# Start and end of a hybrid decoder block: meta rows on another queue, gain in two tiles, the 16-row tile one piece earlier, the last row in quarters

## The chip, the cores and the metric

The kernel runs on one core of one Trainium2 chip. The metric is the device time of one execution in microseconds; the median of three runs of the kernel before is 744.31 us (744.23 to 744.82). The engines are TensorE (PE; its weight loads are listed apart as PEld), VectorE (DVE), ScalarE (ACT), GpSimd (POOL) and SyncE (SP), which only issues transfers. ScalarE has a queue for issuing transfers as well (ACTq). What each engine executes stands in one fixed order; engines wait for each other through semaphores.

## The reference

One decoder block on 1024 tokens of width 1024, with 16 learned meta tokens in front (1040 rows):

```python
h = concatenate([meta, x])                           # 1040 x 1024
h_n = h * rsqrt(mean(h * h) + 1e-6) * norm_g
u, z, q, k, v, za, f, gp, ga = split(h_n @ w_in)     # 8 heads of 64
y_pool = causal_multiscale_pool(u) * silu(z)
y_attn = forgetting_attention(q, k, v, log_sigmoid(f + b)) * silu(za)
merged = sigmoid(gp) * (y_pool @ w_up_pool) + sigmoid(ga) * (y_attn @ w_up_attn)
out = rmsnorm(h + merged @ w_out, final_norm_g)[16:]
```

Everything is float32. The kernel forms each product as three products of high and low parts (`hh`, `hl` of the activations; `whi`, `wlo` of the weights).

## The kernel before, in words

Rows are handled in nine tiles of 128; tile 0 holds the 16 meta rows and the first 112 tokens, and tile 8 the last 16 rows. `norm_load` (L171) brings a tile in on SP's queue; for tile 0 it issues two loads, the tokens and then the meta rows. `norm_stat` (L182) squares a tile on ScalarE, with the sum read out, then `rstd_of` (L110) adds epsilon on VectorE (L113) and raises to the power -0.5 on GpSimd (L114). `norm_scale` (L187) multiplies by that and by the gain on VectorE, in two halves of 512 columns. The gain `norm_g` arrives as one row, `grow`, on ScalarE's queue (L380), and two products of TensorE with a row of ones spread it over 128 partitions into `gb`, one tile of two halves; four warm-up products stand before and one behind. `norm_t` (L192) transposes a tile on TensorE, eight times 128 columns, into `pt` or `pn` in PSUM: there are two `pt` buffers, used in turn, and one `pn`. ScalarE copies the result to `hh` (L212) and VectorE writes the difference to `hl` (L213). Tile 8 takes the short way at L197, L201 and L202: all eight transposes into one `pt` buffer.

The first head pair's q, k and v are then projected in four stretches of tokens, 0 to 256, 256 to 512, 512 to 768, 768 to 1040, in the order q, k, v each: pieces n = 0 to 11 (L431 on). A piece is 24 products in three groups of eight (`hh,whi`, `hl,whi`, `hh,wlo`, L152) into one of three `pj` buffers. Behind or within the pieces stand the remaining tiles' work: which tile is scaled after which piece (L456) and transposed after which (L448) is written out in two tables. For tile 8, square and scale are written behind piece n = 6 and the transposes inside v's piece n = 8, behind its first eight products. q's piece is taken out by four copies on ScalarE (`qa`, L241) and two differences on VectorE (`ql`, L245); k's by L263 and L266.

TensorE's order is the order of the code. At the start, up to L475, the order of the other engines is the code's too. Behind it a scheduler sets theirs. Attention, pooling, gates and output products follow; the last ones (L995) are added to `x` row by row.

At the end each of eight row tiles of 128 collects two halves: `arrive` (L1006) adds a product on VectorE (L1001), squares it on ScalarE (L1015) and sums on GpSimd (L1018, L1021). `store` (L1023) raises to the power on GpSimd (L1026), scales one half on VectorE (L1028) and one on ScalarE (L1031), and issues one transfer for each, on SP's and ScalarE's queue. Two `after` calls, which order without a wait, put each scale behind the last addition or square so far. For row 7 the last half arrives in two quarters of 256 columns, and rows 6 and 7 are stored behind it.

Of the kernel before, what the change touches and what calls it, by code (L numbers as in the profile page):

```python
# [8 lines left out]
F32 = mybir.dt.float32  # L9
# [5 lines left out]
D = 1024  # L15
# [37 lines left out]
def tile_hybrid_block(ctx, tc, x, meta, norm_g, w_in, b_forget, pool_w, pool_scale,  # L53
# [114 lines left out]
    gb = psG.tile([128, 2, 512], F32, name="gb")  # L168
    junk = gp.tile([128, D], F32, name="junk", tag="g")

    def norm_load(i):  # L171
        c0 = i * 128
        n = min(128, L - c0)
        xt = ap_.tile([128, D], F32, name="xt", tag="s", bufs=6)
        if i == 0:
            nc.sync.dma_start(xt[NM:], x2[:128 - NM, :])
            nc.sync.dma_start(xt[:NM], meta)
        else:
            nc.sync.dma_start(xt[:n], x2[c0 - NM:c0 - NM + n, :])
        return xt  # L180

# [5 lines left out]
    def norm_scale(xt, n, r):  # L187
        for j, (c0, c1) in enumerate(HALVES):
            nc.vector.scalar_tensor_tensor(xt[:n, c0:c1], xt[:n, c0:c1], r[:n], gb[:n, j],
# [189 lines left out]
    grow = ap_.tile([1, D], F32, name="grow", tag="t")  # L379
    nc.scalar.dma_start(grow, norm_g)  # L380
    nc.scalar.activation(junk[:1, :2], r32(onesr)[:1, :2], AF.Square)
    xts = {0: norm_load(0), 1: norm_load(1)}
# [7 lines left out]
    for j, (c0, c1) in enumerate(HALVES):  # L390
        nc.tensor.matmul(gb[:, j], r32(onesr)[:1], grow[:, c0:c1], start=True, stop=True)
# [27 lines left out]
    for i in range(2):  # L419
        norm_scale(xts[i], 128, norm_stat(xts[i], 128))  # L420
# [13 lines left out]
    for n, (kind, t0, t1) in enumerate(todo):  # L434
# [4 lines left out]
        elif kind == "k":  # L439
            run(k_piece(0, wk, t0, t1))  # L440
        else:
            g = v_piece(0, wv, t0, t1)
            if n == 8:
# [3 lines left out]
            run(g)  # L447
        i = {0: 2, 1: 3, 3: 4, 4: 5, 6: 6, 7: 7}.get(n)  # L448
# [7 lines left out]
        i = {1: 4, 2: 5, 4: 6, 5: 7, 6: 8}.get(n)  # L456
        if i is not None:
# [548 lines left out]
    def arrive(r, c0, ps):  # L1006
        part, add = plus(r, c0, ps)
        if r not in cnts:
# [6 lines left out]
        marks.append((add, nc.scalar.activation(sq[:, :ps.shape[-1]], part, AF.Square, scale=D ** -0.5,  # L1015
                                                accum_out=sss[r][:, n:n + 1])))
# [6 lines left out]
    def store(r, c):  # L1023
# [4 lines left out]
        after(nc.vector.scalar_tensor_tensor(o[:, a0:a1], xr[r][:, a0:a1], t, fgb[:, a0:a1],  # L1028
                                             op0=ALU.mult, op1=ALU.mult), marks[-1][0])
        nc.sync.dma_start(o2[rr, a0:a1], o[:, a0:a1])  # L1030
        after(nc.scalar.activation(o[:, b0:b1], xr[r][:, b0:b1], AF.Copy, scale=t), marks[-1][1])  # L1031
        nc.scalar.dma_start(o2[rr, b0:b1], o[:, b0:b1])
# [17 lines left out]
    for n in range(7):  # L1050
# [59 lines left out]
```

## Time and profile before

| | us |
|---|---|
| median of 3 runs | 744.31 |
| profiled execution, its own time | 743.96 |
| its span, first to last instruction | 742.2 |
| TensorE busy | 731.2 |
| first projection product starts | 12.11 |
| q's last piece (n = 9) starts | 46.87 |
| last output pass on VectorE starts | 737.69 |

The span is the time between the first and the last instruction that the profiler saw; the execution's own time has 1.76 us around it. A row of a timeline gives the start in us, the time until the last of the merged instructions ends, the engine, the line, the operation, output and inputs by the program's names, shapes, how many were merged and, in brackets, how long the engine stood idle before and what ended that. Starts of instructions that follow each other on an engine can lie up to 0.1 us before the end of the one ahead. Lines are those of the kernel before.

### The profile page before, as it was taken

Reading aid. Unit: us, or ns where it says so; the run is one execution under the profiler, and the core shown is the slowest. Engines: PE = TensorE matmul, PEld = TensorE weight load, DVE = VectorE, ACT = ScalarE, POOL = GpSimd, SP = SyncE. Lnnn points to the kernel's source line nnn. Section 1 sums busy time; section 2 is a strip of 40 time slices with the busy share of each in tenths; the row PEclk is TensorE's granted clock in tenths of the full one; section 3 lists DMA queues with packets and bytes.
Section 4 is the critical chain, followed back from the end, with each engine's and each line's share of the span. In section 5 each row is a group of like instructions: output and inputs, shape, how many; then the busy total and the mean of one; then the engine's idle time right before and its main releaser. Section 6 shows DMA issues by size and latency. Waiting matters only on the chain.

```text
span 742.2 us, 10619 instructions
## 1 busy us (share of the span) xinstructions
PE 731.2 (99%) x3686; PEld 622.7 (84%) x3686; DVE 533.2 (72%) x991; ACT 377.0 (51%) x736; POOL 332.8 (45%) x390
## 2 busy tenths in 40 slices
PE   8999999999999999999999999999999999999996
PEld 5997999988888898889988888888887888888885
DVE  5653577668779877688797687686288554997975
ACT  6662556446557545556563564452545322526445
POOL 4331235456426446345355383183348043606743
PEclk9999999999999999999999999999999999999998
DMA  9301132231312212222323223229375357360006
GB/s 301 88 15 43 29 86 86 62 98 23 95 48 60 80 50 90 78 53 55 94 66 86 80 80 92 72 81 309 95 201 212 142 200 240 116 224 1 1 0 227
DMA packets 76424, 75.35 MB, mean 102 GB/s; under 512 B 9665, under 2 KB 60865, under 8 KB 76370
## 3 DMA queue, kind: packets, MB, share of 16 engines
q1 hardware_dynamic: 74496, 69.95, 30.8%
q10 hardware_dynamic: 1874, 4.72, 1.7%
q8 instruction: 29, 0.48, 0.3%
q14 instruction: 25, 0.20, 0.1%
HBM read 55.58 MB, written 19.07 MB: 101 GB/s over the span
## 4 chain that ended last, share of the span: by engine, by line
PE 87%; DVE 5%; ACT 1%; issue 1%; POOLq 0%; POOL 0%; ACTq 0%
PE pj L152 65%; PE pj L995 8%; PE po L633 5%; PE ps L573 2%; PE ps L572 2%; PE pt L995 2%; PE pj L486 1%; DVE S L612 1%; DVE pl L617 1%; DVE ka L266 0%; PE pj L279 0%; DVE pt L603 0%; ACT S L581 0%; DVE mt L593 0%; ACT whi L140 0%
## 5 line engine op out<-in xcount | busy, mean ns | idle before, releaser
L124 POOL TENSOR_TENSOR wlo<-raw,whi 128x256 fp32r<-128x256 f32 x148 | 121.7, 852 | 192.5 <-ACT whi L140 96.1
L152 PE MATMUL pj<-hh,whi 128*128 128x512 f32 (+4 forms) x768 | 178.4, 360 | 0.6 <-ACT hh L201 0.3
L152 PE MATMUL pj<-hl,whi 128*128 128x512 f32 (+4 forms) x768 | 177.1, 359 | 0.0
L152 PE MATMUL pj<-hh,wlo 128*128 128x512 f32 (+4 forms) x768 | 174.4, 358 | 0.0
L152 PEld LDWEIGHTS pj<-hh,wlo 128*128 128x128 f32 x768 | 132.3, 188 | 18.1
L152 PEld LDWEIGHTS pj<-hh,whi 128*128 128x128 f32 x768 | 131.5, 188 | 18.7 <-ACT hh L201 0.5
L152 PEld LDWEIGHTS pj<-hl,whi 128*128 128x128 f32 x768 | 131.6, 188 | 17.7
L617 DVE TENSOR_TENSOR pl<-S,ph 128x512 fp32r<-128x512 f32 (+4 forms) x112 | 87.1, 792 | 19.3 <-ACT ph L616 18.8
L625 POOL TENSOR_TENSOR acc<-acc,S 128x272 f32<-128x272 f32 (+4 forms) x80 | 76.7, 958 | 11.2 <-ACT S L613 6.0
L581 ACT ACTIVATE S<-ps,negc 128x400 f32<-128x400 f32 (+2 forms) x96 | 49.3, 515 | 44.0 <-DVE S L579 35.7
L613 ACT ACTIVATE S<-S 128x512 f32<-128x512 f32 (+4 forms) x112 | 49.5, 478 | 33.7 <-DVE S L612 33.5
L616 ACT ACTIVATE ph<-S 128x512 fp32r<-128x512 f32 (+4 forms) x112 | 52.2, 480 | 15.8 <-PE po L633 14.4
L588 DVE TENSOR_TENSOR m<-m,S 128x272 f32<-128x272 f32 (+4 forms) x80 | 41.3, 517 | 23.8 <-ACT S L581 22.0
L140 ACT ACTIVATE whi<-raw 128x1024 fp32r<-128x1024 f32 x37 | 39.1, 1056 | 32.2 <-PE pj L152 27.8
L612 DVE TENSOR_TENSOR S<-S,pt 128x512 f32<-128x512 f32 (+4 forms) x112 | 51.9, 498 | 0.8
L836 DVE TENSOR_TENSOR rl<-pj,rl 128x512 f32<-128x512 f32 x32 | 22.0, 689 | 28.0 <-PE pj L152 28.0
L579 DVE SCALAR_TENSOR_TENSOR S<-ps,negc,mask 128x128 f32<-128x128 f32 (+2 forms) x72 | 23.7, 330 | 22.5 <-PE ps L573 22.3
L317 ACT ACTIVATE st<-pj 128x512 f32<-128x512 f32 x40 | 23.7, 593 | 28.1 <-PE pj L152 18.6
L633 PE MATMUL po<-pl,V 128*128 128x512 f32 (+4 forms) x112 | 37.6, 336 | 0.1
L573 PE MATMUL ps<-ql,ka 128*128 128x512 f32 (+4 forms) x112 | 37.5, 334 | 0.0
L572 PE MATMUL ps<-qa,ka 128*128 128x512 f32 (+4 forms) x112 | 36.0, 322 | 0.6 <-ACT S L581 0.5
L995 PE MATMUL pj<-opy 128*128 128x512 f32 (+1 forms) x168 | 36.3, 375 | 0.0
(187 smaller groups left out, 1134.2 us busy)
## 6 DMA issues: line engine op xcount, KB each, us to landing
raw<-in_w_in_dram SPq DMA_DIRECT2D x40, 512.0 KB, 3.9
sp_gp<-st SPq DMA_DIRECT2D x16, 256.0 KB, 2.0
sp_ga<-st SPq DMA_DIRECT2D x16, 256.0 KB, 2.0
rl<-sp_gp SPq DMA_DIRECT2D x8, 512.0 KB, 5.2
rl<-sp_ga SPq DMA_DIRECT2D x8, 512.0 KB, 4.5
W<-in_w_out_dram SPq DMA_DIRECT2D x8, 512.0 KB, 4.8
xr<-in_x_dram SPq DMA_DIRECT2D x8, 512.0 KB, 4.1
xt<-in_x_dram SPq DMA_DIRECT2D x7, 512.0 KB, 8.1
```

Source lines behind the costliest of these rows:

```text
L124: ins = nc.gpsimd.tensor_tensor(out[:, c:c + 256], x[:, c:c + 256], y[:, c:c + 256], op=op)
L152: nc.tensor.matmul(ps, a, b, start=(i == 0), stop=(i == len(seq) - 1))
L572: nc.tensor.matmul(ps[:kb, c0:], ka[:, k0:k0 + kb], qa[:, q0 + c0:q0 + 512], start=True, stop=False)
L573: nc.tensor.matmul(ps[:kb, c0:], ka[:, k0:k0 + kb], ql[:, q0 + c0:q0 + 512], start=False, stop=True)
L581: nc.scalar.activation(s[:kb, f0:], ps[:kb, f0:], AF.Identity, bias=nb_)
L612: nc.vector.tensor_tensor(s[:kb, c0:], s[:kb, c0:], self.pm[:kb, c0:], op=ALU.subtract)
L613: exps.append(nc.scalar.activation(s[:kb, c0:], s[:kb, c0:], AF.Exp))
L616: nc.scalar.activation(ph[:kb, c0:], s[:kb, c0:], AF.Copy)
L617: dves.append(nc.vector.tensor_tensor(pl[:kb, c0:], s[:kb, c0:], r32(ph[:kb, c0:]), op=ALU.subtract))
L625: nc.gpsimd.tensor_tensor(acc[:kb, c0:], acc[:kb, c0:], s[:kb, c0:], op=ALU.add)
L633: nc.tensor.matmul(self.po[:, c0:], v, r[:kb, c0:], start=(b == 0 and i == 0), stop=(b == self.nb - 1 and i == 1))
L995: nc.tensor.matmul(ps, pick(A_, k, p)[:, i * 128:(i + 1) * 128], pick(B_, k, q)[:, c0:c1], start=start and n == 0, stop=n == 11, skip_grou ...
```

## The change

It has five parts.

- The meta rows are loaded from ScalarE's queue, ahead of the gain row, instead of from SP's behind tile 0's tokens.
- The gain is spread into two tiles, so that a half waits for its own product alone.
- Tiles 0 and 1 take a new `norm_stat2`: half of the squares on ScalarE, half on VectorE, both sums added to epsilon in one instruction.
- Tile 8 is squared and scaled behind piece n = 5 with tile 7, and transposed inside k's piece n = 7 behind its first eight products.
- The last quarter of row 7 is squared on VectorE and not marked for the `after` order, and row 7 is stored in four quarters, one issued by ScalarE and three by SP.

```diff
-    gb = psG.tile([128, 2, 512], F32, name="gb")
+    gb = [psG.tile([128, 512], F32, name=f"gb{j}") for j in range(2)]
...
         if i == 0:
+            nc.scalar.dma_start(xt[:NM], meta)
             nc.sync.dma_start(xt[NM:], x2[:128 - NM, :])
-            nc.sync.dma_start(xt[:NM], meta)
...
+    def norm_stat2(xt, n):
+        ss = [sm.tile([128, 1], F32, name="ss") for _ in range(2)]
+        nc.scalar.activation(junk[:n, :512], xt[:n, :512], AF.Square, scale=D ** -0.5, accum_out=ss[0][:n])
+        nc.vector.scalar_tensor_tensor(junk[:n, 512:], xt[:n, 512:], 1.0 / D, xt[:n, 512:], op0=ALU.mult, op1=ALU.mult,
+                                       accum_out=ss[1][:n])
+        r = sm.tile([128, 1], F32, name="rstd", bufs=4)
+        nc.vector.tensor_scalar(r[:n], ss[0][:n], ss[1][:n], EPS, op0=ALU.add, op1=ALU.add)
+        nc.gpsimd.tensor_tensor(r[:n], r[:n], epsp[:n], op=ALU.pow)
+        return r
...
-            nc.vector.scalar_tensor_tensor(xt[:n, c0:c1], xt[:n, c0:c1], r[:n], gb[:n, j],
+            nc.vector.scalar_tensor_tensor(xt[:n, c0:c1], xt[:n, c0:c1], r[:n], gb[j][:n],
...
+    xts = {0: norm_load(0)}
     nc.scalar.dma_start(grow, norm_g)
     nc.scalar.activation(junk[:1, :2], r32(onesr)[:1, :2], AF.Square)
-    xts = {0: norm_load(0), 1: norm_load(1)}
+    xts[1] = norm_load(1)
...
-        norm_scale(xts[i], 128, norm_stat(xts[i], 128))
+        norm_scale(xts[i], 128, norm_stat2(xts[i], 128))
...
         elif kind == "k":
-            run(k_piece(0, wk, t0, t1))
-        else:
-            g = v_piece(0, wv, t0, t1)
-            if n == 8:
+            g = k_piece(0, wk, t0, t1)
+            if n == 7:
                 for _ in range(KO):
                     next(g)
                 norm_t(8, xts[8], ntok(8))
             run(g)
+        else:
+            run(v_piece(0, wv, t0, t1))
...
-        i = {1: 4, 2: 5, 4: 6, 5: 7, 6: 8}.get(n)
-        if i is not None:
+        for i in {1: (4,), 2: (5,), 4: (6,), 5: (7, 8)}.get(n, ()):
             norm_scale(xts[i], ntok(i), norm_stat(xts[i], ntok(i)))
...
-    def arrive(r, c0, ps):
+    def arrive(r, c0, ps, last=False):
...
+        if last:
+            nc.vector.scalar_tensor_tensor(sq[:, :ps.shape[-1]], part, 1.0 / D, part, op0=ALU.mult, op1=ALU.mult,
+                                           accum_out=sss[r][:, n:n + 1])
+        else:
+            marks.append((add, nc.scalar.activation(sq[:, :ps.shape[-1]], part, AF.Square, scale=D ** -0.5,
+                                                    accum_out=sss[r][:, n:n + 1])))
...
+        step = 256 if r == 7 else 512
+        for d in range(0, 512, step):
+            a, b = slice(a0 + d, a0 + d + step), slice(b0 + d, b0 + d + step)
+            after(nc.vector.scalar_tensor_tensor(o[:, a], xr[r][:, a], t, fgb[:, a], op0=ALU.mult, op1=ALU.mult),
+                  marks[-1][0])
+            nc.sync.dma_start(o2[rr, a], o[:, a])
+            after(nc.scalar.activation(o[:, b], xr[r][:, b], AF.Copy, scale=t), marks[-1][1])
+            (nc.sync if d else nc.scalar).dma_start(o2[rr, b], o[:, b])
...
-                    arrive(7, c0, bb_[h][:, :256])
+                    arrive(7, c0, bb_[h][:, :256], h == 1)
```

The order of instructions, at three places. A row gives the line (of the kernel that it belongs to, so the numbers differ by some ten between the two), the operation, output and inputs, the shape and how many follow each other. First TensorE, from the second half of the first group of k's piece n = 7 on; before:

```order
L152 MATMUL pj<-hh_113,whi 128x256 x4
L152 MATMUL pj<-hl_114,whi 128x256 x4
L152 MATMUL pj<-hl_115,whi 128x256 x4
L152 MATMUL pj<-hh_112,wlo 128x256 x4
L152 MATMUL pj<-hh_113,wlo 128x256 x4
L210 MATMUL pn<-ident,xt 128x128 x4
L210 MATMUL pt<-ident,xt 128x128 x4
L279 MATMUL pj<-ident,vt 128x128 x2
L152 MATMUL pj<-hh_112,whi 128x256 x4
L152 MATMUL pj<-hh_113,whi 128x256 x4
L197 MATMUL pt<-ident,xt 128x16 x8
L152 MATMUL pj<-hl_114,whi 128x256 x4
```

The same stretch now:

```order
L152 MATMUL pj<-hh_113,whi 128x256 x4
L207 MATMUL pt<-ident,xt 128x16 x8
L152 MATMUL pj<-hl_114,whi 128x256 x4
L152 MATMUL pj<-hl_115,whi 128x256 x4
L152 MATMUL pj<-hh_112,wlo 128x256 x4
L152 MATMUL pj<-hh_113,wlo 128x256 x4
L220 MATMUL pn<-ident,xt 128x128 x4
L220 MATMUL pt<-ident,xt 128x128 x4
L289 MATMUL pj<-ident,vt 128x128 x2
```

Tile 8's eight transposes have moved ahead of tile 7's (`pn` and `pt`), so that the `pt` buffer they take is the first of tile 6's two; tile 7 then takes the second.

Next VectorE over the same time, from tile 7's sum and scale on (`rstd`, `xt`); before:

```order
L113 TENSOR_SCALAR rstd<-ss 128x1
L189 SCALAR_TENSOR_TENSOR xt<-xt,rstd,gb 128x512 x2
L245 SCALAR_TENSOR_TENSOR ql<-pj,qa 64x256 x2
L213 TENSOR_TENSOR hl_114<-pt,hh_112 128x4x128
L213 TENSOR_TENSOR hl_115<-pt,hh_113 128x4x128
L113 TENSOR_SCALAR rstd<-ss 16x1
L189 SCALAR_TENSOR_TENSOR xt<-xt,rstd,gb 16x512 x2
L266 TENSOR_TENSOR ka<-pj,ka 64x256 x2
```

And now:

```order
L113 TENSOR_SCALAR rstd<-ss 128x1
L199 SCALAR_TENSOR_TENSOR xt<-xt,rstd,gb_119 128x512
L199 SCALAR_TENSOR_TENSOR xt<-xt,rstd,gb_120 128x512
L113 TENSOR_SCALAR rstd<-ss 16x1
L199 SCALAR_TENSOR_TENSOR xt<-xt,rstd,gb_119 16x512
L199 SCALAR_TENSOR_TENSOR xt<-xt,rstd,gb_120 16x512
L255 SCALAR_TENSOR_TENSOR ql<-pj,qa 64x256 x2
L223 TENSOR_TENSOR hl_114<-pt,hh_112 128x4x128
L223 TENSOR_TENSOR hl_115<-pt,hh_113 128x4x128
L212 TENSOR_TENSOR hl_114<-pt,hh_112 128x4x16
L212 TENSOR_TENSOR hl_115<-pt,hh_113 128x4x16
L276 TENSOR_TENSOR ka<-pj,ka 64x256 x2
```

Tile 8's sum and scale now stand ahead of q's `ql` and of tile 6's `hl` (the two rows with 128x4x128), and its own `hl` ahead of k's.

Last the end of VectorE, from row 5's last addition on; before:

```order
L1001 TENSOR_TENSOR xr<-pj,xr 128x512
L1028 SCALAR_TENSOR_TENSOR o<-xr,sst,fgb 128x512
L1001 TENSOR_TENSOR xr<-pj,xr 128x512
L1028 SCALAR_TENSOR_TENSOR o<-xr,sst,fgb 128x512
L1001 TENSOR_TENSOR xr<-pj,xr 128x256 x2
L1028 SCALAR_TENSOR_TENSOR o<-xr,sst,fgb 128x512 x2
```

And now:

```order
L1011 TENSOR_TENSOR xr<-pj,xr 128x512
L1045 SCALAR_TENSOR_TENSOR o<-xr,sst,fgb 128x512
L1011 TENSOR_TENSOR xr<-pj,xr 128x512
L1045 SCALAR_TENSOR_TENSOR o<-xr,sst,fgb 128x512
L1011 TENSOR_TENSOR xr<-pj,xr 128x256
L1045 SCALAR_TENSOR_TENSOR o<-xr,sst,fgb 128x512
L1011 TENSOR_TENSOR xr<-pj,xr 128x256
L1026 SCALAR_TENSOR_TENSOR sq,sso<-xr 128x256
L1045 SCALAR_TENSOR_TENSOR o<-xr,sst,fgb 128x256 x2
```

Row 6's output pass has moved between row 7's two additions, the square of the last quarter (L1026) is new on this engine, and row 7's output comes in two passes of 256 columns.

More of the change, by code (lines that the diff above doesn't have):

```diff
@@ L390, in tile_hybrid_block @@
     for j, (c0, c1) in enumerate(HALVES):
-        nc.tensor.matmul(gb[:, j], r32(onesr)[:1], grow[:, c0:c1], start=True, stop=True)
+        nc.tensor.matmul(gb[j], r32(onesr)[:1], grow[:, c0:c1], start=True, stop=True)
     warm_up(WARM[1])
```

7 lines of the change are left out of this document (removed).

## The prediction

> **What bounds the kernel now.** I read the page's busy line first, then busy time by stretches, then each engine's timeline around the places that the diff touches, and the chain of waits at the end. The page, and two stretches (columns: stretch, its length, busy time of TensorE's products, its weight loads, VectorE, ScalarE and GpSimd, granted clock, DMA share, GB/s):
>
> ```profile
> span 742.2 us, 10619 instructions
> PE 731.2 (99%) x3686; PEld 622.7 (84%) x3686; DVE 533.2 (72%) x991; ACT 377.0 (51%) x736; POOL 332.8 (45%) x390
> ```
>
> ```profile
> 40.00:48.00 8.00, 7.17 (x58) 6.40 (x58) 6.56 (x17) 3.90 (x12) 0.54 (x1) 1.00 0.00 0
> 48.00:55.00 7.00, 7.00 (x58) 7.00 (x58) 1.66 (x5) 4.64 (x9) 4.37 (x7) 1.00 0.08 12
> ```
>
> TensorE is busy 731.2 of 742.2 us, so it is the bound, and only what makes it wait counts. Of its 11 idle us 0.83 lie between 40 and 48 us and nearly all others before the first projection and behind the last product. Right after 48 us it runs gapless: a delay made ahead of that meets no slack to be won back from. TensorE's rows around those 0.83 us, with tile 8, of 16 rows, at L197:
>
> ```profile
> 37.04 1.03 PE L210 MATMUL pt<-ident,xt 128*128 128x128 f32 x8
> 37.83 1.20 PE L152 MATMUL pj<-hh,whi 128*128 128x256 f32 x8
> 38.87 1.11 PE L152 MATMUL pj<-hl,whi 128*128 128x256 f32 x8
> 39.82 1.11 PE L152 MATMUL pj<-hh,wlo 128*128 128x256 f32 x8
> 40.77 0.60 PE L210 MATMUL pn<-ident,xt 128*128 128x128 f32 x4
> 41.35 0.66 PE L210 MATMUL pt<-ident,xt 128*128 128x128 f32 x4
> 41.84 0.38 PE L279 MATMUL pj<-ident,vt 128*128 128x128 f32 x2
> 41.98 1.19 PE L152 MATMUL pj<-hh,whi 128*128 128x256 f32 x8
> 43.42 0.39 PE L197 MATMUL pt<-ident,xt 16*128 16x16 f32 x4 [0.26 <-issue]
> 44.04 0.42 PE L197 MATMUL pt<-ident,xt 16*128 16x16 f32 x4 [0.22 <-DVE xt L189]
> 44.38 1.20 PE L152 MATMUL pj<-hl,whi 128*128 128x256 f32 x8
> 45.42 1.10 PE L152 MATMUL pj<-hh,wlo 128*128 128x256 f32 x8
> 46.87 1.37 PE L152 MATMUL pj<-hh,whi 128*128 128x272 f32 x8 [0.34 <-ACT hh L201]
> ```
>
> At 37.04 TensorE transposes tile 6 into both `pt` buffers. At 37.83 it starts k's piece (n = 7), at 41.98 v's (n = 8). Tile 8's transposes stand inside v's piece and wait 0.26 and 0.22 us for its scale; q's last piece waits 0.34 us for its copy. VectorE and ScalarE beside it:
>
> ```profile
> 38.40 1.41 DVE L189 SCALAR_TENSOR_TENSOR xt<-xt,rstd,gb 128x512 f32<-128x512 f32 x2 [0.66 <-POOL rstd L114]
> 39.72 0.85 DVE L245 SCALAR_TENSOR_TENSOR ql<-pj,qa 64x256 fp32r<-64x256 f32 x2
> 40.60 1.29 DVE L213 TENSOR_TENSOR hl<-pt,hh 128x512 fp32r<-128x512 f32 x2
> 41.80 0.13 DVE L113 TENSOR_SCALAR rstd<-ss 16x1 f32<-16x1 f32 x1
> 42.59 1.39 DVE L189 SCALAR_TENSOR_TENSOR xt<-xt,rstd,gb 16x512 f32<-16x512 f32 x2 [0.65 <-POOL rstd L114]
> ```
>
> ```profile
> 37.44 1.54 ACT L241 ACTIVATE qa<-pj 64x256 fp32r<-64x256 f32 x4
> 39.00 1.09 ACT L212 ACTIVATE hh<-pt 128x512 fp32r<-128x512 f32 x2
> 39.97 1.04 ACT L184 ACTIVATE junk<-xt 16x1024 f32<-16x1024 f32 x1
> ```
>
> **The change, part by part.**
>
> *The tile of 16 rows* is the large term. Its square, scale and transposes move up one piece: the transposes now stand behind the first eight products of n = 7, at 37.83 + 1.20 = 39.03. They need a `pt` buffer as well as the scaled rows. Tile 6 holds both, and the first comes free when VectorE has written `hl` of tile 6, first half; in the old order that was long done. In the new one VectorE scales tile 8 ahead of q's `ql` and of tile 6's `hl`. The new chain, from the rows:
> - ScalarE: tile 8's square (1.04) takes q's place at 37.44; q's copies start at 38.48, tile 6's `hh` 1.56 later, at 40.04. VectorE gets there later still.
> - VectorE: tile 7's scale ends at 38.40 + 1.41 = 39.81, tile 8's sum (0.13) at 39.94. From the sum's end to the scale, with GpSimd's power between, 41.93 to 42.59 was 0.66: the scale runs from 40.60 to 41.99. VectorE idles through the 0.66 with `ql` and `hl` queued behind.
> - `ql` (0.85) ends at 42.84, the first half of `hl` (1.29 / 2) at 43.49, and TensorE starts some 0.1 later, **43.6**.
>
> So TensorE stalls 4.57 us, in a place where it ran without a gap, and everything on it is queued behind: the rest of k's piece, tile 7's transposes, v, q. Given back are the 0.83 us of old gaps, and some of what hides in a broken stream: a group of eight occupies 1.20 but the next follows after 1.04, so each break drains some 0.15, and the old order broke at two places more; tile 7's transposes also paid 41.98 - 40.77 = 1.21 with the values' two, where tile 7's `pt` half then waited for the same `hl`. 4.57 - 0.83 = 3.74; less 0.3 and some 0.2: 3.2. I take **+3.4**. The copies of tiles 7 and 8 are done before q needs them, since TensorE is now the late one.
>
> *The start.* One row of ScalarE's queue, three of TensorE, three of VectorE:
>
> ```profile
> 0.79 0.53 ACTq L380 DMA_DIRECT2D grow<-in_norm_g_dram  x1
> ...
> 3.31 3.78 PE L391 MATMUL gb<-grow,onesr 1*128 1x512 f32 x4
> 7.02 0.80 PE L387 MATMUL pn<-onesr 128*128 128x512 f32 x1
> 7.99 1.97 PE L210 MATMUL pt<-ident,xt 128*128 128x128 f32 x8 [0.17 <-DVE xt L189]
> ...
> 7.19 1.41 DVE L189 SCALAR_TENSOR_TENSOR xt<-xt,rstd,gb 128x512 f32<-128x512 f32 x2 [1.31 <-PE gb L391]
> 8.66 0.15 DVE L113 TENSOR_SCALAR rstd<-ss 128x1 f32<-128x1 f32 x1
> 9.49 1.41 DVE L189 SCALAR_TENSOR_TENSOR xt<-xt,rstd,gb 128x512 f32<-128x512 f32 x2 [0.68 <-POOL rstd L114]
> ```
>
> Two gain tiles let tile 0's first half be scaled before 7.19, but TensorE's order still holds the second gain product (to 7.09) and a warm-up (7.02 + 0.80 = 7.82) ahead of the transposes: 7.85 instead of 7.99, and not on the path. That is tile 1's, scaled at 9.49. Half of its square now stands on VectorE behind tile 0's second half, which still waits for the second gain product: 7.19 + 0.70 + 0.74 (a pass over 512 columns, half of 1.41 and the overlap) = 8.63, where the sum came at 8.66. So nothing is won; ScalarE's shorter half buys nothing. Against it, `grow` now leaves ScalarE's queue behind the meta rows, up to 0.53 later, and the gain products wait for it; at 3.31 they followed straight on the warm-up, so part of that is covered. Ends: -0.53, an issue by the first row (SP's loads go out one issue earlier, tile 1's with them), and +0.53. I take **+0.1**, nearest to the unmoved 8.66.
>
> *The end.* VectorE's last three rows, one each of GpSimd and ScalarE, and SP's stores (shortest, median, longest issue in ns):
>
> ```profile
> 735.73 0.42 DVE L1001 TENSOR_TENSOR xr<-pj,xr 128x256 f32<-128x256 f32 x1 [1.01 <-PE pj L995]
> 736.07 0.74 DVE L1028 SCALAR_TENSOR_TENSOR o<-xr,sst,fgb 128x512 f32<-128x512 f32 x1
> 737.69 0.75 DVE L1028 SCALAR_TENSOR_TENSOR o<-xr,sst,fgb 128x512 f32<-128x512 f32 x1 [0.88 <-POOL sst L1026]
> ...
> 734.66 0.55 POOL L1026 TENSOR_TENSOR sst<-sst,epsp 128x1 f32<-128x1 f32 x1
> ...
> 736.51 0.19 ACT L1015 ACTIVATION_READ_ACCUMULATOR sq<-xr 128x1 f32 x1
> ...
> L1030 SPq DMA_DIRECT2D out_dram<-o x8: 332/332/344, 724.5 to 738.5; - x8
> ```
>
> Row 6's output pass now stands on VectorE ahead of row 7's last addition: ready at 734.66 + 0.55 = 735.21, it runs until 735.98, so the addition starts at 735.98 instead of 735.73. The square follows on the same engine; at the addition's 0.42 for 256 columns it ends at 736.82, where ScalarE's ended at 736.70. From there to the last scale took 0.99 (to 737.69); the last scale so starts about 0.1 later. Then the first two quarters leave half a pass (0.37) earlier, but SP issues three of the four at 0.33 each, so the last one goes out at about 0.75 + 0.33 + 0.1 = 1.2 into the tail where the last halves went at 0.8, with half their bytes. Ends: -0.8 (half a pass, and half of the last transfer) and +0.5 (the late start and an issue more, with a landing that doesn't shrink). I take **-0.2**.
>
> Sum: 3.4 + 0.1 - 0.2 = **+3.3 us**. The profiled execution took 743.96 (span 742.2), so 747.3; the median of the runs shown is 744.31, 0.35 above it, so **747.6**.
>
> **Rivals.**
>
> *The array falls back to its slow speed during the stall.* Eight 128-column transposes took 1.97 us at 7.99 and 1.03 at 37.04: TensorE has two speeds, though the granted clock stands at full in both places, and the slow one is where it starts. The longest wait of TensorE from 12.2 us on is 0.6, so no row tells whether 4.57 us bring it back (waits: total, times, longest):
>
> ```profile
> PE pt L210 <- PE pj L152: 0.6, 1, 0.6
> ```
>
> Price: the two groups of eight that finish k's piece at double time, 0.95 each (38.87 to 39.82): +1.9, so 749.5. Chance 0.20. By the Trainium skill, TensorE: Matmul & The Clock Gate, Part 1 (The HAM clock gate), an idle window of about 3.4 us halves the array's clock until it has been busy for as long; the windows run freely, so, as an estimate from that page, a stall of 4.57 us holds a whole one about once in three and then costs some 1.7 us. No run here shows it so far.
>
> *Not slower.* If `hl` of tile 6 were written before 39.03, the transposes would fit in without a stall, the old 0.83 us would be gone, and with the other terms the time would be 743.4. VectorE's chain would have to be 4.5 us shorter; for it speaks only that a stretch of 0.66 in it is idle. Against it: `hl` ended at 41.9 even without tile 8's work ahead of it. Chance 0.05.
>
> *A shorter wait.* If the transposes found a free buffer and waited for tile 8's scale alone (41.99), the stall would be 3.0, the term 1.8 and the time 746.0. Against it: both `pt` buffers hold tile 6. Chance 0.05.
>
> *The gain row late by the full 0.53*, and the quarters costing their +0.5: 748.7. Chance 0.06.
>
> **How the numbers follow.** Forecast 0.64, with its own range 746.9 to 748.4 (3.2 to 3.74, and half of the small terms' ends). The clock case reaches above, the short wait below: 746.2 to 749.9 leaves out the not-slower case and far ends. What a measurement of this kernel can tell from no change is about 0.2%, 1.5 us. Slower by more: 0.64 + 0.20 + 0.06 and a little of the short wait's, 0.91; within it 0.05; faster 0.04.
>
> **What will show it.** Right: a gap on TensorE of about 4.5 us behind the first eight products of n = 7, put down to VectorE's `hl`; tile 8's scale near 40.6; no gap before q's last piece, which starts near 50.3; the first projection at 12.1 to 12.3. The clock case: groups of eight near 2 us right behind the gap. Wrong: transposes of 16 columns at 39 to 40 us, or a first projection before 11.7.

## The result

The changed kernel takes 750.77 us (median of six runs, 750.23 to 751.52) where the kernel before takes 744.27 in the same comparison: ratio 1.0088, 95% interval 1.0077 to 1.0099, so 0.9% slower. The forecast was 747.6 with a range to 749.9: the direction came out, the size did not. The profiled execution of the changed kernel has a time of its own of 750.91 us, 6.95 above that of before; the two spans differ by 7.0.

The head of its page:

```profile
span 749.2 us, 10631 instructions
...
PE 733.5 (98%) x3686; PEld 626.5 (84%) x3686; DVE 537.7 (72%) x998; ACT 376.5 (50%) x735; POOL 333.0 (44%) x390
```

TensorE is busy 2.3 us longer with the same 3686 products, and idle 15.7 instead of 11.0 us: some of the loss is waiting, and some is products that take longer. Its rows in the start, then around the moved tile (start, time, engine, line, operation, shapes, count, idle time ahead and what ended it):

```profile
5.04 3.78 PE L402 MATMUL gb<-grow,onesr 1*128 1x512 f32 x4 [1.65 <-DMA grow<-in_norm_g_dram]
...
14.03 2.24 PE L152 MATMUL pj<-hh,whi 128*128 128x240 f32 x8
...
40.00 1.20 PE L152 MATMUL pj<-hh,whi 128*128 128x256 f32 x8
45.62 1.03 PE L207 MATMUL pt<-ident,xt 16*128 16x16 f32 x8 [4.41 <-DVE hl L223]
46.58 2.08 PE L152 MATMUL pj<-hl,whi 128*128 128x256 f32 x8
48.45 1.91 PE L152 MATMUL pj<-hh,wlo 128*128 128x256 f32 x8
50.16 1.03 PE L220 MATMUL pn<-ident,xt 128*128 128x128 f32 x4
...
54.52 1.16 PE L152 MATMUL pj<-hh,whi 128*128 128x272 f32 x8
```

Three losses stand here. The gain products wait 1.65 us for the gain row, start at 5.04 instead of 3.31, and k's piece (n = 7) starts at 40.00 instead of 37.83: 2.17 later. Tile 8's transposes wait 4.41 us for `hl` of tile 6. And the two groups of eight behind that wait start 1.87 and 1.71 apart (46.58, 48.45, 50.16), where they stood 0.95 apart before. q's last piece (n = 9) starts at 54.52 instead of 46.87, 7.65 later, while the span is 7.0 longer; the difference of some 0.6 lies within what single profiles scatter by (last column of the table below).

The wait is the one worked out beforehand. VectorE's rows, each within 0.2 us of where it was worked out to stand, once the start's 2.17 us are added:

```profile
40.56 1.41 DVE L199 SCALAR_TENSOR_TENSOR xt<-xt,rstd,gb 128x512 f32<-128x512 f32 x2 [0.66 <-POOL rstd L114]
...
42.67 1.39 DVE L199 SCALAR_TENSOR_TENSOR xt<-xt,rstd,gb 16x512 f32<-16x512 f32 x2 [0.65 <-POOL rstd L114]
43.99 0.85 DVE L255 SCALAR_TENSOR_TENSOR ql<-pj,qa 64x256 fp32r<-64x256 f32 x2
44.87 1.29 DVE L223 TENSOR_TENSOR hl<-pt,hh 128x512 fp32r<-128x512 f32 x2
```

What follows it was only a rival: the clock. The stretches of the changed kernel around the wait (stretch, length, busy time of TensorE's products, weight loads, VectorE, ScalarE, GpSimd, granted clock, DMA share, GB/s):

```profile
40.80:44.21 3.41, 0.41 (x4) 0.20 (x2) 2.76 (x6) 2.58 (x8) 0.54 (x1) 1.00 0.00 0
44.21:47.62 3.41, 2.00 (x13) 1.97 (x14) 2.29 (x6) 0.45 (x2) 0.00 (x0) 0.50 0.00 0
47.62:51.04 3.42, 3.42 (x18) 3.42 (x18) 0.06 (x1) 0.63 (x2) 0.00 (x0) 0.50 0.00 0
```

From 44.21 to 51.04 the granted clock is at half. Transposes and products in it take double: the transposes and two groups from 45.62 to 50.16 occupy 4.54 us, where the same work takes 2.58 in a run whose clock stayed up (shown below, 44.30 to 46.88). That is 2.0 us; tile 7's transposes behind them, still partly at half clock, lose some 0.4 more (50.16 to 51.60, against 46.88 to 47.89 there).

The start on VectorE, whose rows of before stand in the prediction:

```profile
7.23 0.75 DVE L199 SCALAR_TENSOR_TENSOR xt<-xt,rstd,gb 128x512 f32<-128x512 f32 x1 [1.26 <-PE gb L402]
8.85 0.75 DVE L199 SCALAR_TENSOR_TENSOR xt<-xt,rstd,gb 128x512 f32<-128x512 f32 x1 [0.88 <-PE gb L402]
9.51 0.69 DVE L185 SCALAR_TENSOR_TENSOR junk<-xt 128x512 f32<-128x512 f32 x1
...
11.20 1.41 DVE L199 SCALAR_TENSOR_TENSOR xt<-xt,rstd,gb 128x512 f32<-128x512 f32 x2 [0.68 <-POOL rstd L189]
```

Both halves of tile 0's scale wait for a gain product, tile 1's half square stands behind the second half, and tile 1's scale starts at 11.20 instead of 9.49.

The end, VectorE's last rows, and one row of before that the prediction does not show:

```profile
741.25 0.42 DVE L1011 TENSOR_TENSOR xr<-pj,xr 128x256 f32<-128x256 f32 x1
742.19 0.75 DVE L1045 SCALAR_TENSOR_TENSOR o<-xr,sst,fgb 128x512 f32<-128x512 f32 x1 [0.52 <-POOL sst L1040]
742.86 0.42 DVE L1011 TENSOR_TENSOR xr<-pj,xr 128x256 f32<-128x256 f32 x1
...
744.82 0.88 DVE L1045 SCALAR_TENSOR_TENSOR o<-xr,sst,fgb 128x256 f32<-128x256 f32 x2 [0.99 <-POOL sst L1040]
```

```profile
734.29 0.42 DVE L1001 TENSOR_TENSOR xr<-pj,xr 128x256 f32<-128x256 f32 x1
```

From row 7's first addition to the end of the span: 742.2 - 734.29 = 7.91 us before, 749.2 - 741.25 = 7.95 after. By these two profiles the end is worth nothing in either direction: row 6's output pass stands ahead of the last addition, which comes 1.61 us behind the first instead of 1.44, and the last stage takes back about as much (last scale to the end: 4.51 before, 4.38 after).

### The profile page after: what moved, and what is told of

Same layout as the page of the kernel before. It is cut to its first block, busy times and chain, and to the rows that moved or that the text cites. A ratio compares the mean times of both kernels' runs of the same rounds, so it can differ in the third digit from the quotient of the medians.

```text
span 749.2 us, 10631 instructions
## 1 busy us (share of the span) xinstructions
PE 733.5 (98%) x3686; PEld 626.5 (84%) x3686; DVE 537.7 (72%) x998; ACT 376.5 (50%) x735; POOL 333.0 (44%) x390
## 4 chain that ended last, share of the span: by engine, by line
PE 89%; DVE 4%; issue 1%; ACT 0%; POOL 0%; POOLq 0%; DVEq 0%; ACTq 0%
PE pj L152 67%; PE pj L1005 8%; PE po L643 5%; PE ps L583 3%; PE ps L582 2%; PE pt L1005 2%; PE pj L496 1%; DVE S L622 1%; PE pj L289 0%; DVE pl L627 0%; DVE ql L255 0%; DVE m L598 0%; DVE mx L607 0%; DVE ka L276 0%; DVE pt L613 0%
## 5 line engine op out<-in xcount | busy, mean ns | idle before, releaser
L627 DVE TENSOR_TENSOR pl<-S,ph 128x512 fp32r<-128x512 f32 (+4 forms) x112 | 89.4, 813 | 18.3 <-ACT ph L626 17.7
```

The lines of the kernel that those rows point to most:

```text
L627: dves.append(nc.vector.tensor_tensor(pl[:kb, c0:], s[:kb, c0:], r32(ph[:kb, c0:]), op=ALU.subtract))
```

## The experiments

Twelve further kernels ran, and all compute the reference. A ratio is that of a kernel's time to the time of before measured beside it, with its 95% interval in brackets. Besides the times, two distances are read from each profile, since they separate the places: when TensorE starts k's piece n = 7 ("n7"), and from there to the start of q's last piece ("n7 to n9").

| kernel | n7 | n7 to n9 | n9 to end of span |
|---|---|---|---|
| before | 37.83 | 9.04 | 695.3 |
| changed | 40.00 | 14.52 | 694.7 |
| all of the change but tile 8 | 40.02 | 9.04 | 695.5 |
| tile 8's move alone | 38.59 | 14.02 | 695.4 |
| the same, the wait filled with products | 38.68 | 12.12 | 695.3 |
| the same, transposes into another buffer | 39.16 | 11.97 | 695.3 |
| the same, rows scaled well ahead | 37.97 | 11.56 | 694.7 |
| changed, gain row ahead of the meta rows | 39.92 | 14.88 | 695.3 |
| meta rows on ScalarE's queue alone | 40.58 | 9.02 | 695.2 |
| changed without tile 8, meta rows on SP's queue | 38.59 | 9.03 | 696.0 |
| gain row on SP's queue, meta rows on ScalarE's | 37.71 | 9.03 | 694.8 |
| tile 8's statistics early | 38.89 | 8.30 | 695.6 |
| tile 8's rows scaled well ahead | 38.63 | 7.84 | 695.7 |
| the best parts together | 37.42 | 8.10 | 694.6 |

The last column moves by 1.4 us with no relation to the edits; of single profiles, differences under about 1 us in n7 say little either. The start code of before ran in seven of these kernels, with n7 from 37.83 to 39.16.

### Which part costs what

Tile 8 back in its old place, everything else as changed:

```diff
-            g = k_piece(0, wk, t0, t1)
-            if n == 7:
+            run(k_piece(0, wk, t0, t1))
+        else:
+            g = v_piece(0, wv, t0, t1)
+            if n == 8:
...
-        for i in {1: (4,), 2: (5,), 4: (6,), 5: (7, 8)}.get(n, ()):
+        i = {1: 4, 2: 5, 4: 6, 5: 7, 6: 8}.get(n)
+        if i is not None:
```

> The changed kernel with tile 8's scale back behind n = 6 and its transposes back inside n = 8; the other four parts stay. Theory A (start and tile 8 each lose time and add up: 2.1 and 5.4 with 0.5 won back later): 750.8 - 5.0 = 745.8 to 746.3, no half clock after 17 us. Rival B (the late start makes the tile-8 stall worse, or the later slack absorbs the start's loss by itself): 744.3 to 745.0.

746.33 us against 744.7 for before: ratio 1.0022 [1.0013, 1.0031], +1.6 us. The start and the end together cost that much, where the prediction had -0.1.

And tile 8's move alone, in the kernel before:

```diff
-            run(k_piece(0, wk, t0, t1))
-        else:
-            g = v_piece(0, wv, t0, t1)
-            if n == 8:
+            g = k_piece(0, wk, t0, t1)
+            if n == 7:
...
-        i = {1: 4, 2: 5, 4: 6, 5: 7, 6: 8}.get(n)
-        if i is not None:
+        for i in {1: (4,), 2: (5,), 4: (6,), 5: (7, 8)}.get(n, ()):
```

> The kernel before with the tile-8 move alone. Theory A (stall of 4.4 to 4.6 behind the first eight products of n = 7, then half clock for some 5 us): 744.3 + 5.0 = 749.3, last piece of q at about 52.2 instead of 46.87, granted clock 0.5 for 5 to 7 us. Rival B (the half clock in the changed kernel came by the chance of where its window fell): the same stall, clock 1.00 throughout, 747.6.

749.98 us: ratio 1.0074 [1.0057, 1.0091], +5.3. The two parts add up to 6.9, the whole change to 6.5; within the intervals they add up, so nothing here shows that one part makes the other worse. TensorE in this run, and its stretches:

```profile
44.21 1.03 PE L197 MATMUL pt<-ident,xt 16*128 16x16 f32 x8 [4.42 <-DVE hl L213]
45.17 2.08 PE L152 MATMUL pj<-hl,whi 128*128 128x256 f32 x8
```

```profile
38.36:41.77 3.41, 1.44 (x13) 1.23 (x11) 2.09 (x5) 3.35 (x8) 1.09 (x2) 1.00 0.00 0
41.77:45.18 3.41, 0.97 (x9) 0.93 (x9) 2.94 (x6) 0.27 (x1) 0.00 (x0) 0.50 0.00 0
```

The same wait, and the same slow group behind it (2.08 instead of 1.20). The clock fell at 41.77, 2.0 us after TensorE had gone idle at 39.79: the 3.41 us ahead of the fall still hold 1.44 us of products.

### The wait and the clock apart

Tile 8's move alone again, with 18 warm-up products ahead of the transposes. They write the buffer `pn`, which nothing reads then: extra work that leaves the result alone and keeps TensorE busy through the wait.

```diff
                 for _ in range(KO):
                     next(g)
+                warm = psG.tile([128, 4, 128], F32, name="pn")
+                warm_up(18)
                 norm_t(8, xts[8], ntok(8))
```

> As e3 (the kernel before with the tile-8 move alone), with 18 products of ones by ones, 128 x 512, into the free pn buffer between the first eight products of n = 7 and tile 8's transposes; their result is never read. They take about 18 x 0.23 = 4.2 us of a stall of 4.5. Theory A (the half clock comes of the idle array and costs about 2 us on top of the stall): clock 1.00 throughout, tile 8's transposes at the same time as in e3, groups of eight behind them at a pitch of 0.95 instead of 1.9, time 2.0 us below e3. Rival B (what runs slowly behind the stall does so for its operands or for tile 8's products): groups stay near 1.9 and the time is that of e3 or above.

747.37 us: ratio 1.0035 [1.0022, 1.0048], +2.7.

```profile
39.72 4.29 PE L387 MATMUL pn<-onesr 128*128 128x512 f32 x18
44.30 0.67 PE L197 MATMUL pt<-ident,xt 16*128 16x16 f32 x8 [0.29 <-DVE hl L213]
44.90 1.21 PE L152 MATMUL pj<-hl,whi 128*128 128x256 f32 x8
...
46.88 0.60 PE L210 MATMUL pn<-ident,xt 128*128 128x128 f32 x4
```

The transposes start no earlier, but the groups behind them run at full speed. Filling the wait with work that nobody needs makes this kernel 2.6 us faster by the medians (749.98 to 747.37); in the two profiles n7 to n9 shrinks by 1.9. So of tile 8's 5.3 us the wait is some 2.7, and the clock 1.9 to 2.6.

What the transposes wait for, the rows or the buffer: tile 8's move alone, with the transposes in `pn`, which tile 5 left long ago.

```diff
-            both = psT.tile([128, KO, n], F32, name="pt")
+            both = psG.tile([128, KO, n], F32, name="pn")
```

> The kernel before with only tile 8 moved into k's piece, but its transposes write the spare buffer pn, which tile 5 left long ago, so they wait for tile 8's scaled rows alone (in the run that moved it alone: scale from 41.27 to 42.66, first half of hl written at 44.12). Buffer theory (the wait of 4.42 us was tile 6's hl): the wait shrinks by about 1.5, to 2.9 us, and is put down to VectorE's scale. Rival, the wait was for the scaled rows all along: it stays at 4.4. On the clock: if 2.9 idle us are still enough to halve it, as 4.42 were, the time is 744.4 + 2.9 - 0.8 + 2.6 less 0.3 of drained gaps = 748.8 and the groups behind the wait are near 2 us; if a window has to be nearly all idle, no halving, 746.2. A mishap of its own may add up to 0.5: tile 7's first half needs pn next and waits for tile 8's copies.

747.62 us: ratio 1.0044 [1.0032, 1.0057], +3.3 by the ratio and +3.0 by the medians, where 748.8 with a lower clock and 746.2 without were expected.

```profile
42.68 0.39 PE L197 MATMUL pn<-ident,xt 16*128 16x16 f32 x4 [2.32 <-issue]
43.30 0.41 PE L197 MATMUL pn<-ident,xt 16*128 16x16 f32 x4 [0.23 <-DVE xt L189]
43.64 1.47 PE L152 MATMUL pj<-hl,whi 128*128 128x256 f32 x8
```

```profile
41.01:44.42 3.41, 1.51 (x14) 1.41 (x15) 2.71 (x7) 1.79 (x5) 0.54 (x1) 1.00 0.00 0
44.42:47.83 3.41, 3.41 (x18) 3.41 (x17) 1.45 (x5) 1.10 (x4) 0.00 (x0) 0.50 0.00 0
```

The wait shrinks from 4.42 to 2.32 and 0.23, and the second part is put down to the scaled rows: in the change it was the buffer that set its end. The clock falls all the same, in this profile for one stretch of 3.41 us instead of two, which fits a price between the two that were expected.

The converse, rows ready and buffer not: tile 8's load, square and scale put into idle stretches far ahead (that edit is the second under "What the experiments point to"), and then its transposes moved as the change moves them:

```diff
-            run(k_piece(0, wk, t0, t1))
+            g = k_piece(0, wk, t0, t1)
+            if n == 7:
+                for _ in range(KO):
+                    next(g)
+                norm_t(8, xts[8], ntok(8))
+            run(g)
```

> The same kernel (tile 8's rows scaled well ahead), with its transposes moved into k's piece as the change has them. Buffer theory: the rows are long ready, yet the transposes wait for the first half of tile 6's hl, which without tile 8's work on VectorE is written at about 41.2 on the clock of the profile of before (39.72 + 0.85 + 0.65): a stall of 2.1 us put down to hl. n = 7 to n = 9 then takes 8.1 + 2.1 = 10.2, and 0.6 to 1.2 more if the clock is halved for one window; time 745.7 to 746.9. Rival (the rows' lateness was the cost): no stall, 743.6.

746.72 us: ratio 1.0038 [1.0024, 1.0051], where the same kernel with the transposes in their old place has 742.87 against the same runs of before.

```profile
41.49 0.66 PE L201 MATMUL pt<-ident,xt 16*128 16x16 f32 x8 [2.32 <-DVE hl L217]
42.08 1.98 PE L152 MATMUL pj<-hl,whi 128*128 128x256 f32 x8
```

```profile
38.81:42.22 3.41, 1.09 (x13) 0.86 (x12) 3.18 (x6) 1.43 (x4) 0.00 (x0) 1.00 0.00 0
```

With its rows long ready, the tile still waits 2.32 us, for tile 6's `hl` to leave the buffer, as the buffer theory said (2.1). In this order of VectorE's work the place that the change chose costs a wait with the two `pt` buffers, however early the rows are; no run had both the early rows and the transposes in `pn`. And 2.32 us of idling were enough for the clock.

### The start

The gain row ahead of the meta rows on ScalarE's queue, all else as changed:

```diff
-            nc.scalar.dma_start(xt[:NM], meta)
             nc.sync.dma_start(xt[NM:], x2[:128 - NM, :])
+            nc.scalar.dma_start(xt[:NM], meta)
...
-    xts = {0: norm_load(0)}
     nc.scalar.dma_start(grow, norm_g)
+    xts = {0: norm_load(0)}
```

> The changed kernel with the two loads on ScalarE's queue in the other order: the gain row first, then the meta rows. Theory A (the gain row is late because it stands behind the meta rows and tile 0's packets on the transfer engines): the gain products start at 3.3 instead of 5.04, the first projection some 2 us earlier (about 12.0), and the time falls by 2.0 to 748.8. Rival B (taking the meta rows off SP's queue lets tile 1's load start earlier, and its traffic delays the gain row wherever it stands): the gain products still start after 4.5 and the time stays at 750.5 or more. The stall of TensorE at tile 8 and the half clock behind it stay in both.

751.54 us: ratio 1.0088 [1.0073, 1.0103], no better than the change. ScalarE's and TensorE's rows:

```profile
1.35 0.34 ACTq L177 DMA_DIRECT2D xt<-in_meta_tokens_dram  x1
...
6.13 0.63 ACT L184 ACTIVATE junk<-xt 128x512 f32<-128x512 f32 x1 [2.91 <-DMA xt<-in_meta_tokens_dram]
```

```profile
3.32 3.78 PE L402 MATMUL gb<-grow,onesr 1*128 1x512 f32 x4
```

The gain products are back at 3.32, but now the meta rows are late: tile 0's squares wait for them until 6.13, where they started at 4.93 in the changed kernel. Neither expectation had that. Whichever of the two was issued second on ScalarE's queue landed late. Three runs took this apart. The first has the meta rows back on SP's queue, tile 8 in its old place, and everything else of the change:

```diff
-            nc.scalar.dma_start(xt[:NM], meta)
             nc.sync.dma_start(xt[NM:], x2[:128 - NM, :])
+            nc.sync.dma_start(xt[:NM], meta)
```

> The changed kernel with tile 8 in its old place and the meta rows back on SP's queue, so the gain row goes out first again. What stays of the change: two gain tiles, the squares of tiles 0 and 1 on two engines, and the end. Without the queue's move undone it measured 746.33. Queue theory (the 1.6 us came from the gain row, landing 2.5 us later behind the meta rows): gain products at 3.3, tile 1's scale at 9.4, time 744.2 within 0.5. Rival, the split squares or the end cost it: 745.5 to 746.3.

744.42 us: ratio 1.0003 [0.9994, 1.0011]. The split gain tile, the split squares and the end together cost nothing that can be measured, and bring nothing; no run takes these three apart. The second is the kernel before with the meta rows alone moved:

```diff
+            nc.scalar.dma_start(xt[:NM], meta)
             nc.sync.dma_start(xt[NM:], x2[:128 - NM, :])
-            nc.sync.dma_start(xt[:NM], meta)
...
+    xts = {0: norm_load(0)}
     nc.scalar.dma_start(grow, norm_g)
     nc.scalar.activation(junk[:1, :2], r32(onesr)[:1, :2], AF.Square)
-    xts = {0: norm_load(0), 1: norm_load(1)}
+    xts[1] = norm_load(1)
```

> The kernel before with only the meta rows moved to ScalarE's queue, ahead of the gain row. Queue theory: gain products at about 5.0 instead of 3.3, first projection about 1.6 to 1.9 later, time 744.4 + 1.6 = 746.0. Rival, the split squares cost it: 744.4, with the gain row's delay covered.

745.96 us: ratio 1.0019 [1.0010, 1.0027], +1.4.

```profile
5.05 3.77 PE L392 MATMUL gb<-grow,onesr 1*128 1x512 f32 x4 [1.67 <-DMA grow<-in_norm_g_dram]
```

The wait for the gain row is that of the changed kernel (1.65). This one move is the loss of the start, as far as the intervals tell. The third gives each of the two transfers the head of a queue:

```diff
+            nc.scalar.dma_start(xt[:NM], meta)
             nc.sync.dma_start(xt[NM:], x2[:128 - NM, :])
-            nc.sync.dma_start(xt[:NM], meta)
...
-    nc.scalar.dma_start(grow, norm_g)
+    nc.sync.dma_start(grow, norm_g)
+    xts = {0: norm_load(0), 1: norm_load(1)}
     nc.scalar.activation(junk[:1, :2], r32(onesr)[:1, :2], AF.Square)
-    xts = {0: norm_load(0), 1: norm_load(1)}
```

> The kernel before with the gain row first on SP's queue and the meta rows alone on ScalarE's, so that neither is second on ScalarE's queue. Queue theory: gain products at 3.3 as before, and tile 1's rows land early, as in the runs with the meta rows off SP (6.4 instead of 7.5 to 7.9), so that tile 1's scale follows tile 0's at about 9.4 as before or up to 0.4 earlier: 744.4, within 0.4. Rival: 4 KB ahead on SP's queue delay tile 0 by more than half a microsecond, 745.0.

744.24 us: ratio 0.9998 [0.9989, 1.0007]. With the meta rows still on ScalarE's queue and the 4 KB of the gain row ahead of SP's loads the loss is gone: it was not ScalarE's queue as such that cost it, but being issued second there. Place and time of issue move together in these runs (0.79 us for a first transfer, 1.24 and 1.35 for a second).

### What the experiments point to

Tile 8's statistics taken early, its scale and its transposes in their old places:

```diff
-        i = {1: 4, 2: 5, 4: 6, 5: 7, 6: 8}.get(n)
+        i = {1: 4, 2: 5, 4: 6, 5: 7}.get(n)
...
+        if n == 4:
+            r8 = norm_stat(xts[8], ntok(8))
+        if n == 6:
+            norm_scale(xts[8], ntok(8), r8)
```

> The kernel before with one change: tile 8's square, sum and power are taken behind n = 4, where ScalarE idles, and its scale and transposes stay where they were. VectorE then has no 0.65 us of idling ahead of tile 8's scale. If the 0.83 us of gaps on TensorE around n = 8 hang on that stretch, they go and the time is 744.4 - 0.8 = 743.6 (ratio 0.9989). If they hang on the copies of tile 7 and of the values instead, it is 744.4.

743.73 us: ratio 0.9992 [0.9983, 1.0001]; the time alone does not tell it from no change. In the profile n7 to n9 is 8.30 instead of 9.04; a gap of 0.24 stays ahead of q's last piece. Then the load and the scale early as well, one half of the scale while VectorE waits for tile 6's power, the other behind the values' copies (`norm_half` is one half of `norm_scale`):

```diff
-        if n + 4 < 9:
-            xts[n + 4] = norm_load(n + 4)
+        for i in {3: (7, 8)}.get(n, (n + 4,) if n < 3 else ()):
+            xts[i] = norm_load(i)
...
+        if n == 3:
+            r8 = norm_stat(xts[8], ntok(8))
...
-            norm_scale(xts[i], ntok(i), norm_stat(xts[i], ntok(i)))
+            r = norm_stat(xts[i], ntok(i))
+            if n == 4:
+                norm_half(0, xts[8], ntok(8), r8)
+            norm_scale(xts[i], ntok(i), r)
...
             run(v_blocks(0, 2 * (n // 3) - 2, 2 * (n // 3)))
+            if n == 4:
+                norm_half(1, xts[8], ntok(8), r8)
```

> The kernel before with tile 8's load one piece earlier, its square behind n = 3, and the two halves of its scale in stretches where VectorE idles at n = 4 (while GpSimd takes tile 6's power, and behind the values' copies). Transposes stay in n = 8. With only the statistics early, two of the three gaps (0.26 and 0.22 us) went and 0.24 of the third stayed. If that rest hangs on VectorE's queue (tile 8's scale of 1.39 us ahead of tile 7's copies), it goes too: n = 7 to n = 9 takes 8.1 us, against 9.04 before and 8.30 there, and the time is 744.5 - 0.95 = 743.6 (ratio 0.9987). Rival: the last piece waits for the copies of tile 8 by their place behind the values' copies on ScalarE; then 0.24 stays, ratio 0.9990.

742.87 us: ratio 0.9982 [0.9974, 0.9991], 0.2% faster than the kernel before.

```profile
42.77 1.19 PE L152 MATMUL pj<-hh,whi 128*128 128x256 f32 x8
43.89 0.66 PE L201 MATMUL pt<-ident,xt 16*128 16x16 f32 x8
...
46.47 1.16 PE L152 MATMUL pj<-hh,whi 128*128 128x272 f32 x8
```

All three of the old gaps are gone, and n7 to n9 is 7.84, 1.20 less than before. Last, this together with the gain row first on SP's queue, the meta rows on ScalarE's, two gain tiles, tile 0's square on two engines (tile 1's on ScalarE alone), and the change's end:

```diff
-        norm_scale(xts[i], 128, norm_stat2(xts[i], 128))
+        norm_scale(xts[i], 128, (norm_stat2, norm_stat)[i](xts[i], 128))
```

> All that the runs speak for together: tile 8 as in the first kernel of this call, the gain row first on SP's queue and the meta rows on ScalarE's, two gain tiles, tile 0's square on two engines (tile 1's on ScalarE alone, so that its sum isn't queued behind VectorE's half), and the change's end. Worked out: tile 0's scale from 6.65 to 7.97 as with the two gain tiles and the gain row early, tile 1's sum right behind, its scale at 8.9 instead of 9.5: -0.6; tile 8: -0.95; the end: -0.1; 744.5 - 1.65 = 742.9, ratio 0.9978. Rival: TensorE's slow speed in the start, which ends only with a window of the clock gate, takes the 0.6 back: 743.4, ratio 0.9985.

742.03 us: ratio 0.9972 [0.9960, 0.9983], 2.1 us faster than the kernel before by the ratio, and some 8.6 faster than the changed one. VectorE's start:

```profile
6.42 1.46 DVE L203 SCALAR_TENSOR_TENSOR xt<-xt,rstd,gb 128x512 f32<-128x512 f32 x2 [0.67 <-POOL rstd L189]
...
8.62 1.41 DVE L203 SCALAR_TENSOR_TENSOR xt<-xt,rstd,gb 128x512 f32<-128x512 f32 x2 [0.68 <-POOL rstd L114]
```

With the gain row early, two gain tiles and tile 0's half square let its scale start at 6.42 instead of 7.19, and tile 1's at 8.62 instead of 9.49. The two gain tiles and the split square, which brought nothing in the run with the meta rows on SP's queue, let these rows start earlier here; in time this kernel (0.9972) is not told apart from the one with tile 8's rows early alone (0.9982), since the intervals overlap.

## Why the prediction was wrong in size

Two steps of the sum failed. It put the clock behind the wait at nothing, where that took 1.9 to 2.6 us; and it bounded the gain row's delay by the time of one issue, so that the start stood at +0.1, where it took 1.4 to 1.6. By the medians the 6.5 us of the comparison are 2.7 for the wait, 2.6 for the clock, 1.4 to 1.6 for the queue and none for the end. That adds to 6.7 to 6.9, within the intervals of its parts.

**The wait: right.** The stall was put at 4.57 us behind the first eight products of n = 7, ended by `hl` of tile 6; it was 4.41, with every VectorE row of the chain within 0.2 us of where it was worked out to stand. The term of +3.4 measured +2.7 in the time of the run with the filled wait, and +3.1 in its n7 to n9 (12.12 - 9.04). The buffer argument, on which the "shorter wait" rival fell, is shown from both sides by the two runs that free the buffer or the rows.

**The clock: named, with far too small a chance.** The rival had the right mechanism, the right place (the two groups that finish k's piece) and a price of 1.9 against 1.9 to 2.6 measured. Its chance, 0.20, had no row behind it; the estimate that stood beside it, once in three, asked for a whole idle window of 3.4 us inside the wait. That was not needed. In all five profiles with an unfilled wait of 2.3 to 4.4 us the clock fell; in four of them the 3.41 us ahead of its fall still held 0.41, 1.09, 1.44 and 1.51 us of products (the rows of these stretches stand above), in the fifth, the changed kernel with the gain row first, none. By the Trainium skill, TensorE: Matmul & The Clock Gate, Part 1 (The HAM clock gate), the clock goes down after at least one idle window of about 3.4 us. Here, if the window is the 3.41 us ahead of the fall, one that was up to 44% busy was enough (1.51 of 3.41), so the measurement decides against that reading. The section also has the clock come back after a busy window of about 3.4 us, and that agrees in the middle of the kernel: whole records of the clock last 3.41, 6.83, 27.31, 30.72 and 723.63 us, which are 1, 2, 8, 9 and 212 times 3.413, and after each of these falls the clock came back behind the first such window in which TensorE was wholly busy, as in the rows from 47.62 to 51.04 above. Had the clock's case been the forecast, it would have been 749.5, which is 1.3 too low: about what the start took beyond its term.

**The start: +0.1 predicted, +1.4 to 1.6 measured.** The step that failed is the upper end. "Up to 0.53 later" was the time that ScalarE takes to issue one transfer more; the landing was taken as unmoved. The gain row was issued 0.45 later (1.24 instead of 0.79), and its products started 1.73 later (5.04 instead of 3.31) after a wait of 1.65, part of the delay being covered by the warm-up, as said. No row of before showed a transfer second on that queue under SP's loads, so there was no ground for an upper end of 0.53; the nearest row, in the view of before's transfers up to 8 us (line, queue, KB each, us from issue to landing), is the meta rows' own:

```profile
xt<-in_meta_tokens_dram SPq DMA_DIRECT2D x1, 64.0 KB, 3.2
```

With it, an issue at 1.24 and a landing 3.2 later is 4.44: products 1.1 later, and that end belonged into the range. The observation that tile 0's scale, waiting for the gain, holds tile 1's sum on VectorE was right, and it turned the late gain product into a late first projection: 14.03, where 12.1 to 12.3 was given. The split of the square is not needed for that: with the meta rows alone moved, and whole squares, tile 1's scale starts at 11.07 and the first projection at 13.90.

**The end: -0.2 predicted, 0.0 measured.** Row 6's pass does stand ahead of the last addition, and the last scale follows row 7's first addition by 3.57 us instead of 3.40 (0.17 later, 0.1 was given); the quarters give back 0.13, not 0.3. This is read from one profile of each kernel; that the end costs and brings nothing fits the run with the meta rows on SP's queue (1.0003), which has it together with the other parts.

**The rest.** The 0.83 us of old gaps were given back as said: there is no gap ahead of q's last piece in the changed kernel. TensorE being the bound held in every run, and nothing lost ahead of 50 us was won back later, beyond the 1.4 that single profiles scatter by.

## What to carry to other kernels

When work is moved forward on an engine that never idles, two things must be ready: its data and the buffer it writes. The buffer comes free only when the engines that read its old contents are done, and here that reading (`hl` of tile 6) stood in VectorE's order behind other work. A new stall has a second price, the slow clock behind it; in this kernel 2.3 us of idling already brought it, so a wait of such a length is priced with the groups behind it at double time, or filled with work. A small transfer that gates the start wants the head of a queue: issued second, 0.45 us later, the gain row let its products start 1.73 us later here, and the time of one issue is no bound for that.

## What the runs showed of the hardware that was not expected

- The clock halved behind idling of 2.32 us (two runs), not only behind 4.4 (three runs), and for 3.41 or 6.83 us at a time; 18 products that compute nothing, in the wait, kept it at 1.00.
- The start runs at half speed until a moment that differs between kernels with the same start code. That code brought the first projection's first two groups at 2.25 and 1.91 us in one run and at 1.50 and 1.07 in the profile of before:

```profile
12.69 2.25 PE L152 MATMUL pj<-hh,whi 128*128 128x240 f32 x8
14.73 1.91 PE L152 MATMUL pj<-hl,whi 128*128 128x240 f32 x8
```

```profile
12.11 1.50 PE L152 MATMUL pj<-hh,whi 128*128 128x240 f32 x8
13.45 1.07 PE L152 MATMUL pj<-hl,whi 128*128 128x240 f32 x8
```

  The first record of the full clock came at 11.39 us in the profile of before, and between 11.39 and 17.11 in the seven kernels with that start; n7 followed it from 37.83 to 39.16. The profile of before was one of the early ones, so comparing it alone with the changed kernel's can overstate the start's loss: 2.17 against 1.4 to 1.6 by times. The "granted clock 1.00" of the rows ahead of that first record is no measurement: a value filled in where there is no record. So the prediction's remark that the granted clock stands at full at 7.99 as at 37.04 read such a value; the eight transposes there, 1.97 us against 1.03, ran at half speed. With the late gain row the first full clock came at 16.8 to 18.7. What exactly a window must hold for the clock to rise in the start stays open: no one share of busy time fits all the runs.
- Why the transfer that is second on ScalarE's queue lands late, by its place behind the first one or by the load of SP's packets, was not told apart in full; the run with each at the head of a queue shows only that neither is late then. It fits a hand of SP's loads in it that the meta rows, first on ScalarE's queue and issued at 0.79 in both, land 3.3 us later in the changed kernel, where SP's first 448 KB are issued at 0.79 too, and 2.1 us later in the run with each at the head, where these are issued at 1.20. It is not the moving of the first one's bytes alone: with the gain row first, its last packet on ScalarE's queue is through at 1.87 us, and the first packet of the meta rows, issued at 1.35, starts at 3.86. Nor is it the transfer itself: the gain row's packet takes 0.19 us in the changed kernel and 0.16 before, but starts at 4.20 instead of 1.71.
- A pass on VectorE that also sums its squares leaves a second record of 0.08 us, and the sum of two scalars took 0.21 where that of one took 0.15. For tile 0 it takes 1.03 us from the square's start to the sum's end instead of 1.33, so the split of a square saves less than the 0.53 of half a pass.
